# Expert-gather dots moved behind the list decode, and 80 of 128 expert blocks with a spilled first product

## The chip, the cores and the metric

The kernel runs on one core of one Trainium2 chip. The metric is the device time of one execution in microseconds, as the median of several runs. The profile shows one execution, with TensorE as PE (matmuls) and PEld (weight loads), VectorE as DVE, ScalarE as ACT, GpSimd as POOL and SyncE as SP. SP issues all plain DMAs, POOL the indirect ones.

## The reference, cut to what matters

The program is one step of a two-layer streaming encoder on 512 + 32 = 544 tokens of width 1024. Each layer has a mixer (attention, a state-space model, pooling) and then the channel mixer that this case is about, which picks 16 of 16384 experts for each of 8 heads:

```python
def one(xb):
    q = (xb @ w_q).reshape(blk, PEER_HEADS, 2, D_HALF)
    s = jnp.einsum('nhpd,hpkd->nhpk', q, sub_keys, preferred_element_type=jnp.float32)
    sv, si = lax.top_k(s, PEER_TOPK)
    ...
    cv, ci = lax.top_k(cand, PEER_TOPK)
    eid = i1 * N_KEYS + i2
    g = jax.nn.softmax(cv, axis=-1)
    act = jax.nn.gelu(jnp.einsum('nd,nhkd->nhk', xb, u_tab[eid], preferred_element_type=jnp.float32),
                      approximate=False)
    return jnp.einsum('nhk,nhkd->nd', (g * act).astype(xb.dtype), v_tab[eid])
```

So a token takes 128 experts: for each the dot of its row of `u_tab` with the token, a gelu, a gate, and the sum of rows of `v_tab` with these weights.

## The kernel before, in words

Both layers run the same code (`peer`, line 149). After the mixer and `topk` (the choice of experts, most of it on VectorE), the 544 tokens are split.

**The first 128 tokens are gathered.** For each of their 128 experts, one indirect DMA (`gather`, line 267, on POOL) brings 128 rows of 2048 floats, the u row and the v row of one expert per token, into one of three `uv` buffers. VectorE takes the dot of the u half with the tokens (`junk`, line 269), ScalarE the gelu, VectorE multiplies by the gate (line 273) and adds the weighted v half to `accg` (line 275), after which the buffer is free for the next gather.

**The other 416 tokens go through all 16384 experts densely,** in 128 blocks of 128 experts. First the gates are scattered into a dense table G: `gbuild` (the list decode, lines 404 to 421) compares the lists with an iota on VectorE (lines 406 to 411, 52 rounds of four operations of 128x1024), multiplies the one-hot matrices on TensorE (lines 417 and 418, 832 matmuls a layer), and writes G to DRAM in 13 pieces. Then for each block the first product (`upass`, line 146) multiplies the block's u rows with the tokens, in 24 matmuls of 416 columns since both sides are split in a high and a low part (`uh` by ScalarE on line 133, `ul` by VectorE on line 134); the result gets a gelu (lines 175 or 194). The second product (line 217) multiplies the gated activations with the block's v rows, again in 24 matmuls of 416 columns per block.

**Spilled blocks.** The second product needs G, the first does not. So the first `NSPILL` = 56 blocks have their first product computed ahead, while VectorE still chooses and decodes; line 176 writes the activations to the DRAM tensor `AC`. The rest, 72 blocks, are computed in the main loop (lines 184 to 234), which goes over groups of `GB` = 4 blocks, with the 14 spilled groups spread evenly between the 18 others (`order`, line 183). In a group, line 187 loads the gates, line 191 the spilled activations (or `upass` computes them), line 196 applies the gates, lines 198 and 200 split the product in `wh` and `wl`, and the loop over `d` runs the second product in eight pieces of 128 output columns. The sums of four of the eight stay in PSUM to the end; the other four are added to `acc` on VectorE (line 224), four additions a group.

**What sets the order.** A scheduler that runs when the program is built fixes the order of the instructions on each engine; the engines then work in that order. `gstep` (line 254) says how many gathers the program text issues at each place: weight `WSP` per spilled block, `WD1` per spilled group, `WD2` per other group, scaled by `GEARLY` so that the last comes a little before the end. The scheduler may draw a gather's VectorE work ahead of that. At the end `tail_load` (line 244) loads the residual rows into the three `uv` buffers and adds `accg` (line 251), and lines 230 to 234 transpose and add the dense sums.

Of the kernel before, what the change touches and what calls it, by code (L numbers as in the profile page):

```python
# [12 lines left out]
ALU = mybir.AluOpType  # L13
# [7 lines left out]
GB = 4  # L21
# [5 lines left out]
VB, WB = 4, 6  # L27
ACB = 6
UF = 1
GEARLY = 1.08  # L30
NSPILL = 56
WSP = 0.1
WD1 = 1.3
WD2 = 5
GSC = 32768.0
STARTS = [0, 16, 24, 29, 33, 36, 38, 40, 42, 43, 44, 45, 46, 47, 48, 49]
# [6 lines left out]
class Ker:  # L43
# [105 lines left out]
    def peer(s, layer):  # L149
        nc, tc, I = s.nc, s.tc, s.I  # L150
        G = s.dram.tile([ND // 32, 128, 128, 32], F32, name='G')
        AC = s.dram.tile([NSPILL, 128, ND], F32, name='AC')
        with ExitStack() as sc:
# [15 lines left out]
            with ExitStack() as gs:  # L169
                s.gbuild(gs, I1T, I2T, GhT, GlT, G)  # L170
            for b in range(NSPILL):
                ps, = s.upass(I['peer_uT'][layer, b])
                s.gstep(WSP)
                a_ = s.ac.tile([128, ND], F32, name='act')
                nc.scalar.activation(a_, ps[:, :ND], AF.Gelu)
                nc.sync.dma_start(AC[b], a_)
# [3 lines left out]
            hold = [s.psC(), s.psB(), s.psC(), s.psB()]  # L180
            un = list(range(NSPILL, 128, GB))
            sp = list(range(0, NSPILL, GB))
            order = sorted([((i - UF * (i < 2)) / len(un), g) for i, g in enumerate(un)] + [((i + 0.5) / len(sp), g) for i, g in enumerate(sp)])
            for gi, (_, g0) in enumerate(order):
# [3 lines left out]
                for b in range(g0, g0 + GB):  # L188
                    a_ = s.ac.tile([128, ND], F32, name='act')
                    if b < NSPILL:  # L190
                        nc.sync.dma_start(a_, AC[b])
                    else:
                        ps, = s.upass(I['peer_uT'][layer, b])
                        nc.scalar.activation(a_, ps[:, :ND], AF.Gelu)
                    av = a_.rearrange('p (g n) -> p g n', n=32)
                    nc.vector.tensor_mul(av, av, gt[:, :, b - g0, :])  # L196
                    wh = wp.tile([128, ND], F32R, name='wh')
                    nc.scalar.activation(wh, a_, AF.Copy)  # L198
                    wl = wp.tile([128, ND], F32R, name='wl')
                    nc.vector.tensor_sub(wl, a_, wh)  # L200
                    grp.append((wh, wl))
                for d in range(8):
                    s.gstep((WD1 if g0 < NSPILL else WD2) / 8)
                    if d % 4 == 0:
# [20 lines left out]
                    if gi == len(order) - 1:  # L225
# [5 lines left out]
                        for t, m, n in ((1, 2, 128), (3, 1, 128), (4, 1, 32)):  # L231
                            o = xs[(t - 1) // 2].rearrange('p (a b) -> p a b', a=2)[:n, (t + 1) % 2:(t + 1) % 2 + m, d * 128:(d + 1) * 128]
                            i = ps.rearrange('p (a b) -> p a b', b=128)[:n, t - 1:t - 1 + m]
# [18 lines left out]
        return xs  # L252

    def gstep(s, w):
        total = NSPILL * WSP + NSPILL // GB * WD1 + (128 - NSPILL) // GB * WD2
        s.gtot = min(NG, s.gtot + w * GEARLY * NG / total)
        while s.gdone + KP <= s.gtot:
            s.gather(s.layer, s.gdone)
            s.gdone += KP

    def gather(s, layer, s0):
        nc = s.nc
        act = s.small.tile([128, KP], F32, name='gact')
        rows = []
        for i in range(KP):
            uv = s.gp.tile([128, 2048], F32, name='uv')
            nc.gpsimd.indirect_dma_start(out=uv, out_offset=None, in_=s.I['peer_uv'].rearrange('l e d -> (l e) d'), in_offset=bass.IndirectOffsetOnAxis(ap=s.eid[:, s0 + i:s0 + i + 1], axis=0))  # L267
            junk = s.gp.tile([128, 1024], F16, name='junk', bufs=1)
            nc.vector.scalar_tensor_tensor(junk, uv[:, 0:1024], 1.0, s.xg, op0=ALU.mult, op1=ALU.mult, accum_out=act[:, i:i + 1])  # L269
            rows.append(uv)  # L270
        w = s.small.tile([128, KP], F32, name='gw')
        nc.scalar.activation(w, act, AF.Gelu)  # L272
        nc.vector.tensor_mul(w, w, s.gsl[:, s0:s0 + KP])
        for i in range(KP):
            nc.vector.scalar_tensor_tensor(s.accg, rows[i][:, 1024:2048], w[:, i:i + 1], s.accg, op0=ALU.mult, op1=ALU.add)  # L275
# [1211 lines left out]
```

## Time and profile before

| What | Value |
|---|---|
| time, median of 3 runs | 3504.01 us (3503.53 to 3505.63) |
| the profiled execution's own time | 3495.36 us |
| its span, first to last instruction | 3493.3 us |
| PE busy | 3156.7 us (90%) |
| PEld busy | 2987.6 us (86%) |
| DVE busy | 2674.9 us (77%) |
| ACT busy | 1240.8 us (36%) |
| POOL busy | 688.5 us (20%) |
| DMA | 761.07 MB, 218 GB/s over the span |
| mean granted TensorE clock | 0.946 |

The two layers follow each other; the profile's stages of the first layer are the choice of experts (about 350 to 604 us), the decode (604 to 848 us) and the main loop (871 to 1774 us), and the second layer has the same three some 1700 us later. Busy shares over the whole span mix these stages, so the tables by stretch are the ones to read. In the rows, a matmul's duration is longer than the distance to the next, since matmuls are pipelined; the distance is a stretch divided by the number of matmuls in it.

### The profile page before, as it was taken

Reading aid. Unit: us, or ns where it says so; the run is one execution under the profiler, and the core shown is the slowest. Engines: PE = TensorE matmul, PEld = TensorE weight load, DVE = VectorE, ACT = ScalarE, POOL = GpSimd, SP = SyncE. Lnnn points to the kernel's source line nnn. Section 1 sums busy time; section 2 is a strip of 40 time slices with the busy share of each in tenths; the row PEclk is TensorE's granted clock in tenths of the full one; section 3 lists DMA queues with packets and bytes.
Section 4 is the critical chain, followed back from the end, with each engine's and each line's share of the span. In section 5 each row is a group of like instructions: output and inputs, shape, how many; then the busy total and the mean of one; then the engine's idle time right before and its main releaser. Section 6 shows DMA issues by size and latency. Waiting matters only on the chain.

```text
span 3493.3 us, 48079 instructions
## 1 busy us (share of the span) xinstructions
PE 3156.7 (90%) x17932; PEld 2987.6 (86%) x17932; DVE 2674.9 (77%) x5685; ACT 1240.8 (36%) x2213; POOL 688.5 (20%) x436
## 2 busy tenths in 40 slices
PE   6779969993999999999999997799669999999998
PEld 5667868993999999999988786799569999999998
DVE  7975699998888899544455539999988988884544
ACT  3233323443333333333344422344423333333332
POOL 4432012232222222000000400133222222210000
PEclk9889989995999999999999998899779999999999
DMA  3112224998999999645432222379899999984542
GB/s 114 50 44 105 89 86 140 347 344 334 344 329 328 335 348 338 225 159 158 146 101 67 83 87 83 111 266 348 320 335 334 337 336 339 346 287 155 178 144 94
DMA packets 314437, 761.07 MB, mean 218 GB/s; under 512 B 22782, under 2 KB 164318, under 8 KB 277852
## 3 DMA queue, kind: packets, MB, share of 16 engines
q1 hardware_dynamic: 277340, 489.56, 41.3%
q0 software_dynamic: 36864, 268.45, 20.3%
q8 instruction: 140, 2.29, 0.3%
q14 instruction: 93, 0.76, 0.1%
HBM read 667.42 MB, written 90.51 MB: 217 GB/s over the span
## 4 chain that ended last, share of the span: by engine, by line
PE 51%; DVE 21%; issue 12%; DMA 10%; POOL 3%; ACT 2%; SPq 0%; POOLq 0%; ACTq 0%; DVEq 0%
PE psa L146 18%; PE psb L217 11%; PE psc L217 6%; PE psa L217 5%; DMA uv<-in_peer_uv,eid 5%; DMA raw<-in_peer_uv 4%; POOL uv L267 3%; DVE ul L134 3%; PE psa L1013 2%; DVE wl L134 1%; DVE trep L282 1%; DVE accg L275 1%; DVE X L281 1%; DVE X L284 1%; PE psa L1205 1%
## 5 line engine op out<-in xcount | busy, mean ns | idle before, releaser
L146 PE MATMUL psa<-hh,ul 128*128 128x416 f32 (+1 forms) x2304 | 805.8, 354 | 91.7 <-DVE ul L134 91.7
L146 PE MATMUL psa<-hh,uh 128*128 128x416 f32 (+1 forms) x2304 | 807.2, 354 | 10.3 <-ACT uh L133 9.6
L146 PE MATMUL psa<-hl,uh 128*128 128x416 f32 (+1 forms) x2304 | 796.8, 349 | 0.0
L267 POOL DMA_INDIRECT uv<-in_peer_uv,eid x256 | 420.4, 1642 | 1161.4 <-DVE accg L275 1010.0
L134 DVE TENSOR_TENSOR wl<-raw,wh 128x1024 fp32r<-128x1024 f32 (+1 forms) x281 | 343.6, 1224 | 270.7 <-ACT wh L133 270.1
L146 PEld LDWEIGHTS psa<-hh,ul 128*128 128x128 f32 x2304 | 439.5, 192 | 110.1 <-DVE ul L134 104.8
L133 ACT ACTIVATE uh<-raw 128x1024 fp32r<-128x1024 f32 x272 | 287.0, 1057 | 594.6 <-PE psa L146 365.3
L133 ACT ACTIVATE wh<-raw 128x1024 fp32r<-128x1024 f32 (+1 forms) x303 | 316.1, 1049 | 439.6 <-DMA raw<-in_peer_uv 357.5
L146 PEld LDWEIGHTS psa<-hh,uh 128*128 128x128 f32 x2304 | 440.4, 193 | 22.8 <-ACT uh L133 16.2
L146 PEld LDWEIGHTS psa<-hl,uh 128*128 128x128 f32 x2304 | 440.2, 192 | 5.5
L134 DVE TENSOR_TENSOR ul<-raw,uh 128x1024 fp32r<-128x1024 f32 x268 | 339.5, 1269 | 95.5 <-ACT uh L133 95.5
L217 PE MATMUL psb<-wh 128*128 128x416 f32 x1024 | 358.6, 353 | 45.8 <-ACT wh L198 45.8
L217 PE MATMUL psb<-wh,wl 128*128 128x416 f32 x1024 | 358.5, 351 | 0.0
L269 DVE SCALAR_TENSOR_TENSOR junk<-uv,xg 128x1024 f16<-128x1024 f32 x256 | 312.2, 1219 | 59.1 <-DMA uv<-in_peer_uv,eid 58.7
L217 PE MATMUL psb<-wl,wh 128*128 128x416 f32 x1024 | 357.2, 350 | 0.2 <-DVE wl L200 0.2
L275 DVE SCALAR_TENSOR_TENSOR accg<-uv,gw,accg 128x1024 f32<-128x1024 f32 x256 | 327.8, 1281 | 3.0
L217 PEld LDWEIGHTS psb<-wh 128*128 128x128 f32 x1024 | 192.9, 188 | 48.0 <-ACT wh L198 46.4
L198 ACT ACTIVATE wh<-act 128x416 fp32r<-128x416 f32 x256 | 139.0, 548 | 195.1 <-DVE act L196 131.4
L95 POOL TENSOR_TENSOR rs<-ms,nhalf 128x1 f32<-128x1 f32 (+1 forms) x35 | 19.2, 551 | 891.5 <-DVE ms L93 886.6
L217 PEld LDWEIGHTS psb<-wl,wh 128*128 128x128 f32 x1024 | 192.3, 188 | 2.6 <-DVE wl L200 0.4
L217 PEld LDWEIGHTS psb<-wh,wl 128*128 128x128 f32 x1024 | 192.1, 188 | 1.9
L272 ACT ACTIVATE gw<-gact 128x1 f32<-128x1 f32 x256 | 51.4, 201 | 373.0 <-DVE junk L269 372.3
(548 smaller groups left out, 5963.0 us busy)
## 6 DMA issues: line engine op xcount, KB each, us to landing
raw<-in_peer_uT SPq DMA_DIRECT2D x256, 512.0 KB
raw<-in_peer_uv SPq DMA_DIRECT2D x256, 512.0 KB
G<-st SPq DMA_DIRECT2D x26, 2048.0 KB
gt<-G SPq DMA_DIRECT2D x64, 832.0 KB
AC<-act SPq DMA_DIRECT2D x112, 208.0 KB
act<-AC SPq DMA_DIRECT2D x112, 208.0 KB
raw<-in_w_out SPq DMA_DIRECT2D x16, 512.0 KB
raw<-in_peer_wq SPq DMA_DIRECT2D x16, 512.0 KB
```

What stands on the lines that cost most here:

```text
L133: nc.scalar.activation(hi, raw, AF.Copy)
L134: (eng or nc.vector).tensor_sub(lo, raw, hi)
L146: nc.tensor.matmul(pss[i][:, :c - a], w[:, k, :], x[:, k, a:c], start=(k == 0 and j == 0), stop=(k == 7 and j == 2))
L198: nc.scalar.activation(wh, a_, AF.Copy)
L217: nc.tensor.matmul(ps[:, :ND], w[:, d % 4 * 128:(d % 4 + 1) * 128], x, start=(first and q == 0 and j == 0), stop=(last and q == GB - 1 and ...
L267: nc.gpsimd.indirect_dma_start(out=uv, out_offset=None, in_=s.I['peer_uv'].rearrange('l e d -> (l e) d'), in_offset=bass.IndirectOffsetOnA ...
L269: nc.vector.scalar_tensor_tensor(junk, uv[:, 0:1024], 1.0, s.xg, op0=ALU.mult, op1=ALU.mult, accum_out=act[:, i:i + 1])
L272: nc.scalar.activation(w, act, AF.Gelu)
L275: nc.vector.scalar_tensor_tensor(s.accg, rows[i][:, 1024:2048], w[:, i:i + 1], s.accg, op0=ALU.mult, op1=ALU.add)
L281: nc.vector.max_index(idx[:, 0:8], val[:, 0:8], src)
L282: nc.vector.match_replace(out=w[:n], in_to_replace=val[:, 0:8], in_values=src, imm_value=-3e38)
L1013: nc.tensor.matmul(ps[:n, :], l, ww, start=(k == 0 and i == 0), stop=(k == 7 and i == 2))
```

## The change

Three things change. The gathers' dot is put behind the most recent `wl` of the second product in VectorE's program order (`issue_after` adds an order between two instructions of one engine; no wait comes with it), where `s.gate` is set by each block of the main loop: a gather whose call stands in a group's loop has its dot behind that group's last `wl`. No gather is called in the spill loop any more, so `WSP` is gone. And 80 blocks instead of 56 are spilled, so that the main loop has 20 spilled groups and 12 others; the weights `WD1` and `GEARLY` change with it: 128 x 1.05 / 92 = 1.46 gathers per unit of weight, 2.3 per spilled group and 7.3 per other group, against 1.21, 1.6 and 6.1 before.

```diff
-GEARLY = 1.08
-NSPILL = 56
-WSP = 0.1
-WD1 = 1.3
+GEARLY = 1.05
+NSPILL = 80
+WD1 = 1.6
 WD2 = 5
...
             for b in range(NSPILL):
                 ps, = s.upass(I['peer_uT'][layer, b])
-                s.gstep(WSP)
                 a_ = s.ac.tile([128, ND], F32, name='act')
...
                     wl = wp.tile([128, ND], F32R, name='wl')
-                    nc.vector.tensor_sub(wl, a_, wh)
+                    s.gate = nc.vector.tensor_sub(wl, a_, wh).ins
                     grp.append((wh, wl))
...
     def gstep(s, w):
-        total = NSPILL * WSP + NSPILL // GB * WD1 + (128 - NSPILL) // GB * WD2
+        total = NSPILL // GB * WD1 + (128 - NSPILL) // GB * WD2
...
             junk = s.gp.tile([128, 1024], F16, name='junk', bufs=1)
-            nc.vector.scalar_tensor_tensor(junk, uv[:, 0:1024], 1.0, s.xg, op0=ALU.mult, op1=ALU.mult, accum_out=act[:, i:i + 1])
+            with s.tc.issue_after(s.gate):
+                nc.vector.scalar_tensor_tensor(junk, uv[:, 0:1024], 1.0, s.xg, op0=ALU.mult, op1=ALU.mult, accum_out=act[:, i:i + 1])
```

The changed kernel's own line numbers are one or two lower than those before. Three places show how the instructions move.

VectorE in the list decode of the first layer, before. The lines 406 to 411 are the decode, `ul` the low part of a block's u rows, `junk`, `gw` and `accg` a gather's dot, gate and sum:

```order
L406 TENSOR_TENSOR A<-iota_83,i1t 128x1024
L408 TENSOR_TENSOR B<-iota_83,i2t 128x1024
L410 TENSOR_TENSOR Ah<-A,ght 128x1024
L134 TENSOR_TENSOR ul<-raw,uh 128x1024
L269 SCALAR_TENSOR_TENSOR junk,gact<-uv,xg 128x1024
L275 SCALAR_TENSOR_TENSOR accg<-uv,gw,accg 128x1024
L410 TENSOR_TENSOR Ah<-A,ght 128x1024
L411 TENSOR_TENSOR A<-A,glt 128x1024
L406 TENSOR_TENSOR A<-iota_83,i1t 128x1024
L408 TENSOR_TENSOR B<-iota_83,i2t 128x1024
L134 TENSOR_TENSOR ul<-raw,uh 128x1024
```

The same stage in the changed kernel:

```order
L405 TENSOR_TENSOR A<-iota_83,i1t 128x1024
L407 TENSOR_TENSOR B<-iota_83,i2t 128x1024
L133 TENSOR_TENSOR ul<-raw,uh 128x1024
L410 TENSOR_TENSOR A<-A,glt 128x1024
L409 TENSOR_TENSOR Ah<-A,ght 128x1024
L405 TENSOR_TENSOR A<-iota_83,i1t 128x1024
L407 TENSOR_TENSOR B<-iota_83,i2t 128x1024
L405 TENSOR_TENSOR A<-iota_83,i1t 128x1024
L407 TENSOR_TENSOR B<-iota_83,i2t 128x1024
L410 TENSOR_TENSOR A<-A,glt 128x1024
L409 TENSOR_TENSOR Ah<-A,ght 128x1024 x2
```

Between the first and the last of the 208 decode operations there stood 31 `ul`, 29 dots and 28 sums; now there are 25 `ul` and no gather work. In both kernels 31 `ul` of dense blocks stand ahead of the decode.

VectorE from the end of the decode to the first gathers of the main loop, before (the last rows of a run of gathers, then the first group's gates, line 196, and low parts, line 200):

```order
L269 SCALAR_TENSOR_TENSOR junk,gact<-uv,xg 128x1024
L273 TENSOR_TENSOR gw<-gw,gsl 128x1
L275 SCALAR_TENSOR_TENSOR accg<-uv,gw,accg 128x1024
L196 TENSOR_TENSOR act<-act,gt 128x416 x4
L200 TENSOR_TENSOR wl<-act,wh 128x416 x4
L269 SCALAR_TENSOR_TENSOR junk,gact<-uv,xg 128x1024
L273 TENSOR_TENSOR gw<-gw,gsl 128x1
L275 SCALAR_TENSOR_TENSOR accg<-uv,gw,accg 128x1024
```

And in the changed kernel, where 27 first products follow the last decode operation:

```order
L410 TENSOR_TENSOR A<-A,glt 128x1024
L133 TENSOR_TENSOR ul<-raw,uh 128x1024 x27
L194 TENSOR_TENSOR act<-act,gt 128x416
L133 TENSOR_TENSOR wl<-raw,wh 128x1024
L198 TENSOR_TENSOR wl<-act,wh 128x416
...
L133 TENSOR_TENSOR ul<-raw,uh 128x1024 x2
L194 TENSOR_TENSOR act<-act,gt 128x416
L198 TENSOR_TENSOR wl<-act,wh 128x416
L268 SCALAR_TENSOR_TENSOR junk,gact<-uv,xg 128x1024 x2
```

All 128 gathers of a layer now have their dot in the main loop; before, 34 of them stood ahead of the first gate.

SP's queue where `tail_load` reads the residual rows into the `uv` buffers, in the first layer. Before, five such loads (line 250) stood among loads of u and v rows for groups that were still to come:

```order
L132 DMA raw<-in_peer_uv 128x2x512
L250 DMA uv<-XR 128x1024
L132 DMA raw<-in_peer_uT 128x1024
L250 DMA uv<-XR 128x1024 x2
L132 DMA raw<-in_peer_uT 128x1024
L250 DMA uv<-XR 128x1024
L250 DMA uv<-XR 32x1024
```

Now they stand at the very end, the first of them ahead of the last v load of the layer (`w_ckv` is a weight of the next layer):

```order
L131 DMA raw<-in_peer_uv 128x2x512 x4
L248 DMA uv<-XR 128x1024
L131 DMA raw<-in_peer_uv 128x2x512
L131 DMA raw<-in_w_ckv 128x576
L248 DMA uv<-XR 128x1024 x2
L131 DMA raw<-in_w_ckv 128x576 x2
L248 DMA uv<-XR 128x1024
L248 DMA uv<-XR 32x1024
```

## Rows read from the trace of the kernel before

**Rows 1.** The page: the granted TensorE clock in 40 slices of the span.

```profile
PEclk9889989995999999999999998899779999999999
```

**Rows 2.** By stretch: busy PE, PEld, DVE, ACT, POOL (instructions), clock, DMA share, GB/s.

```profile
640.00:680.00 40.00, 39.81 (x294) 36.30 (x293) 39.53 (x62) 18.66 (x35) 10.42 (x4) 1.00 0.96 363
790.00:830.00 40.00, 17.62 (x152) 14.43 (x149) 38.91 (x62) 15.91 (x30) 8.08 (x5) 0.57 0.89 349
830.00:870.00 40.00, 8.52 (x78) 7.47 (x78) 31.05 (x49) 7.26 (x18) 10.52 (x9) 0.57 0.89 327
```

**Rows 3.** Who waited for whom, 790 to 870 us: total, times, longest.

```profile
PE psb L418 <- DVE A L411: 12.7, 6, 3.9
```

**Rows 4.** VectorE's groups, 604 to 870 us: count, busy us, mean ns, idle before.

```profile
L275 DVE SCALAR_TENSOR_TENSOR accg<-uv,gw,accg 128x1024 f32<-128x1024 f32 x34 | 43.5, 1279 | 0.2
L269 DVE SCALAR_TENSOR_TENSOR junk<-uv,xg 128x1024 f16<-128x1024 f32 x34 | 41.5, 1220 | 12.9 <-DMA uv<-in_peer_uv,eid 12.9
L134 DVE TENSOR_TENSOR ul<-raw,uh 128x1024 fp32r<-128x1024 f32 x32 | 38.9, 1218 | 1.5 <-ACT uh L133 1.5
L406 DVE TENSOR_TENSOR A<-iota,i1t 128x1024 f16<-128x1024 f16 x52 | 35.6, 685 | 0.4 <-PE psc L381 0.4
```

**Rows 5.** POOL's gathers, 604 to 870 us.

```profile
L267 POOL DMA_INDIRECT uv<-in_peer_uv,eid x37 | 77.5, 2096 | 186.8 <-DVE accg L275 139.8 <-DVE gw L273 46.2 <-issue 0.8
```

**Rows 6.** First products: PE's groups, 340 to 604 us; spill gelus, first and last start.

```profile
L146 PE MATMUL psa<-hh,ul 128*128 128x416 f32 x234 | 88.8, 382 | 42.7 <-DVE ul L134 42.7
...
L175 ACT ACTIVATE act<-psa x56: 493/500/539, 411.6 to 764.9; 128x416 f32<-128x416 f32 x56
```

**Rows 7.** PE's groups, 604 to 790 us.

```profile
L146 PE MATMUL psa<-hh,ul 128*128 128x416 f32 x247 | 89.9, 365 | 1.9 <-DVE ul L134 1.9
...
L417 PE MATMUL psb<-Ah,B 128*128 128x128 f16 x183 | 28.3, 220 | 0.0
...
L417 PE MATMUL psc<-Ah,B 128*128 128x128 f16 x121 | 19.6, 220 | 0.0
```

**Rows 8.** The main loop by stretch, columns as in rows 2.

```profile
1500.00:1600.00 100.00, 100.00 (x531) 98.99 (x531) 48.30 (x65) 31.40 (x42) 0.00 (x0) 1.00 0.52 164
950.00:1400.00 450.00, 446.88 (x2355) 441.12 (x2355) 400.30 (x598) 158.31 (x274) 111.51 (x78) 1.00 0.93 336
1000.00:1100.00 100.00, 98.23 (x510) 96.38 (x510) 86.11 (x130) 35.48 (x61) 25.67 (x17) 0.98 0.93 330
```

**Rows 9.** First and last start of PE's instructions of lines 146 and 217, first layer.

```profile
L146 PE MATMUL psa<-hh,ul x544: 344/352/552, 874.2 to 1734.1; 128*128 128x416 f32 x182
L217 PE MATMUL psb<-wh x512: 344/352/716, 870.9 to 1767.5; 128*128 128x416 f32 x171
L217 PE MATMUL psa<-wh,wl x256: 344/353/356, 882.0 to 1773.5; 128*128 128x416 f32 x128
```

**Rows 10.** Groups of POOL and VectorE, 950 to 1400 us.

```profile
L267 POOL DMA_INDIRECT uv<-in_peer_uv,eid x78 | 112.3, 1440 | 338.6 <-DVE accg L275 317.7 <-DMA uv<-in_peer_uv,eid 7.9 <-DVE gw L273 7.3
...
L269 DVE SCALAR_TENSOR_TENSOR junk<-uv,xg 128x1024 f16<-128x1024 f32 x78 | 95.1, 1219 | 9.8 <-DMA uv<-in_peer_uv,eid 9.8
...
L134 DVE TENSOR_TENSOR wl<-raw,wh 128x1024 fp32r<-128x1024 f32 x63 | 76.8, 1220 | 13.5 <-ACT wh L133 13.3
...
L196 DVE TENSOR_TENSOR act<-act,gt 128x416 f32<-128x416 f32 x64 | 36.8, 586 | 2.7 <-ACT act L194 1.5 <-DMA act<-AC 1.1
```

**Rows 11.** DMA queues and issues: count and KB each.

```profile
q0 software_dynamic: 36864, 268.45, 20.3%
...
raw<-in_peer_uv SPq DMA_DIRECT2D x256, 512.0 KB
...
gt<-G SPq DMA_DIRECT2D x64, 832.0 KB
...
act<-AC SPq DMA_DIRECT2D x112, 208.0 KB
```

**Rows 12.** The residual loads of the first layer's end: first and last start.

```profile
L250 SPq DMA_DIRECT2D uv<-XR x5: 320/339/428, 1405.7 to 1415.6; - x5
```

## The prediction

> **What bounds the kernel now.** I read the page first, for the stages: the clock row has low places in the mixers and where experts are chosen, and its lowest once per layer behind that, slice 10 and again slices 29 and 30 [rows 1]. The table by stretch shows what happens in that later place. At 640 to 680 us TensorE and VectorE are both full (39.81 and 39.53 of 40 us). From 790 on VectorE stays at 38.91 of 40 us while TensorE falls to 17.62, then 8.52, at a granted clock of 0.57, so between its levels of 1.2 and 2.4 GHz and nearer the lower one [rows 2]. TensorE has run out of first products: the last spill gelu starts at 764.9 us [rows 6]. It waits for the decode's operands from VectorE [rows 3], and the main loop can't begin before G is written; its first second product is at 870.9 us [rows 9]. What holds the decode up is seen in VectorE's groups: beside 208 decode operations (four lines of 52 at 0.685 us, 142 us) and 32 `ul` it does 34 dots of 1.220 us and 34 sums of 1.279 us, 85 us of gather work [rows 4].
>
> In the main loop TensorE is the bound: 531 matmuls in 100 us, or 0.188 us each and 4.52 us per block and product, with weight loads at 98.99% [rows 8]. There the gathers cost nothing: at 950 to 1400 us, with 78 of them, TensorE is busy 446.88 of 450 us [rows 8, 10]. After some 1410 us they are used up (the residual loads that take over their buffers start at 1405.7 us [rows 12]), VectorE falls to half busy and the DMA from 336 to 164 GB/s [rows 8]. So the gathers run too early: they slow the stage that starves TensorE and are missing where they would be free.
>
> **The change, part by part,** for the first layer; the second has the same stages.
>
> *Decode.* It begins at 604 us, unchanged: 31 `ul` stand ahead of it in both orders. By then 3 x 234 matmuls are done, 29.25 blocks [rows 6]. VectorE now has 142 us of decode and 25 `ul` at 1.218, 30 us: 173 us if nothing overlaps [rows 4]. TensorE has 25 blocks at 4.52, 113 us, and 832 decode matmuls. From 604 to 790 us it did about 3 x 247 large ones, 139 us, and 2 x (183 + 121) = 608 small ones (line 418 has as many as line 417) in the remaining 47 us, so at most 0.078 us each and 65 us for 832: 178 us [rows 7]. I take 175 us, an end at 779 instead of 848. Bounds: 161 us, as VectorE's durations overlapped by some 7% in the full stretch before, and 190 us, if the two engines wait for each other.
>
> The Trainium skill, page "Perfetto Trace Analysis", section "Identifying the Most-Contended Engine", holds matmul busy time to be a poor measure of TensorE's headroom and goes by the weight loads' share. The stretch at 640 to 680 us shows 39.81 us busy but 36.30 of weight loads, 91% [rows 2]. By that rule TensorE has slack in the decode, VectorE's 161 us alone would hold, and the total would be some 28 us lower than by my 175.
>
> *First products behind it.* G is written while TensorE goes on with spilled blocks. Ahead of the first gate stand 83 `ul`; with 84 blocks done (80 and the first group) TensorE has 84 - 29.25 - 25 = 29.75 blocks left, 134 us: the main loop begins at 913 us, 42 later than now, but with 24 blocks less in it. 30 us of this cover G's last writes and the first loads, which today lie open.
>
> *Main loop.* Before, 196 block products (3 x 544 matmuls are 68 blocks, and 128 second products) took from 870.9 to the last start at 1773.5 us, 902.6 us or 4.605 each, all its small stalls included [rows 9]. Now 44 + 128 = 172 are left: 792 us, to 1705 us. This holds if VectorE and the DMA keep up.
> VectorE: per second product a `wl` of the weights, a gate, a low part and an addition, 1.220 + 3 x 0.586 = 2.98 us; 128 x 2.98 + 44 x 1.22 + 128 gathers x (1.22 + 1.28 + 0.16 for gate and read-out) = 381 + 54 + 340 = 775 us, 98% of 792. At 950 to 1400 us the same sum is 63 x 2.98 + 36 `ul` x 1.22 + 78 x 2.66 = 439 of 450, also 98%, with TensorE full [rows 8, 10].
> DMA: 48 u loads and 128 v loads of 0.524 MB, 32 gate loads of 0.852, 80 spilled activations of 0.213, 128 gathers of 268.45/256 = 1.049 MB: 271 MB in 792 us, 342 GB/s against 336 [rows 8, 11].
> Gather ring: three buffers turned over one gather in 450/78 = 5.77 us [rows 10]; needed are 792/128 = 6.19.
> So the loop now runs all along at the load of its present busiest part. Bounds: 172 x 4.52 = 778 us, or 271 MB at the 330 GB/s of the slowest of its stretches, 821 us [rows 8].
>
> *Spill traffic and gate.* 24 more writes and reads of 0.213 MB are 10 MB a layer; the writes lie beside first products alone, where little else moves, the reads are in the sum above. The gate is an order within VectorE's own queue and costs nothing by itself. Behind a dot that waits for its rows stand gates and low parts that TensorE needs: that is the second rival. POOL's queue keeps its order; the first three gathers land before the loop and then wait.
>
> *End of a layer.* The residual loads now need buffers that the last gathers free, on SP ahead of the last v load, and line 251 stands ahead of the final additions. Before they had 350 us of room [rows 12]. No row prices this; it lies between 0 and one turn of the ring, 3 x 5.77 = 17 us. I take 8, nearer the middle, since the loop ends with half a group of products already loaded.
>
> **Sum.** Per layer: 604 + 175 + 134 + 792 + 8 = 1713 against 1773 us (the last start of before), 60 us less, 120 for both. The profiled execution took 3495.4 us, 8.6 under the median; 3375 on its scale is **3384 us** as a median. A measurement of this kernel can tell about 0.2%, 7 us, from no change.
>
> **The rivals.** *The transfers become the bound.* For it: the main loop asks for 342 GB/s from end to end, in its first 95% (`GEARLY` 1.05) about 350, and the DMA share is already 0.93 [rows 8]; loads of v and gates come twice as often among spilled groups. Against it: the decode stretch moved 363 GB/s [rows 2]. At 821 us per loop each layer gains 31 us: 3442 us; with a late decode (190 us) and a full turn of the ring at the end 7 us: 3490. The Trainium skill, page "DMA: Bandwidth & Descriptors", section "Specifications", gives about 358 GB/s of HBM per core; 350 would just fit under it, and the 363 here is above it.
>
> *The ring becomes the bound, and the kernel slower.* Gathers now have only the main loop, and VectorE stops at each dot whose rows are late, with the gates of the next group behind it; TensorE then idles and loses its clock as at 790 us. Price: beside the decode a gather took 266/37 = 7.2 us [rows 5]; 128 of them are 920 us, 128 over 792, so a layer is 68 us slower and the time 3640 us. It decides from (1773 - 8 - 913)/128 = 6.66 us per gather. Against it: at the loop's own mix it was 5.77, with 9.8 us of waits for rows in 450 us [rows 10].
>
> *The decode doesn't get shorter,* because TensorE or ScalarE's evictions set its 244 us and the gathers only filled gaps: then 848 + 134 + 792 + 8 = 1782, 9 us slower per layer, 3522 us. For it: TensorE reads as full at 640 us. Against it: after 790 us TensorE is idle and VectorE still full, and the decode goes no faster [rows 2, 3].
>
> **How the numbers follow.** Forecast 65%, transfers 20%, ring 4%, no shorter decode 4%, and 7% for the forecast's lower bounds together (161, 778 and 0 us: 36 us per layer more, 3312 us). The first two and the last are faster by more than 0.2%, less 2% for a long decode and slow transfers that add up to nothing: faster 0.90, same 0.02, slower 0.08. The range leaves out half of the transfers' upper part, the two slow rivals and the extreme low end: **3322 to 3450 us**.
>
> **What would show it.** The decode's last operation near 780 us, with no dot before it; TensorE full from 604 us on at a granted clock of 1; the first second product near 913 us; about 17 gathers in each 100 us up to the end of the loop, near 1705 us; DMA near 342 GB/s there. Wrong would be: TensorE idle in the main loop behind dots that wait for rows, or behind loads of v rows; a main loop over 850 us; a decode that still ends near 848 us.

## The result, and the profile after

The changed kernel takes 3351.93 us (median; 3346.45 to 3355.85), the kernel before 3504.82 us beside it (3503.53 to 3507.74): the ratio is 0.9566, with a 95% interval of 0.955 to 0.9582. That is 153 us less. The forecast was 3384 us in a range of 3322 to 3450, so 120 us less. The execution that was profiled took 3355.85 us, 139.5 us less than the profiled execution of before.

All lines after the change stand one or two lower than before: the dot is line 268, the gather 265, the sum 274, the decode's four VectorE operations are 405 to 410, the first product is 145, the second 215, the splits 132 and 133. First the page: the slices of the granted clock.

```profile
PEclk8889988999999999999999999899999999999999
```

Slices 10, 29 and 30, at 5, 7 and 7 tenths before [rows 1], are now at 9. What stands there now, by stretch of the first layer (columns as in rows 2): the decode, the first products behind it, the main loop; below them the main loop's 450 us that rows 8 show for before.

```profile
608.00:772.00 164.00, 163.63 (x1393) 150.31 (x1392) 155.83 (x237) 88.48 (x160) 7.80 (x4) 1.00 0.77 283
780.00:904.00 124.00, 124.00 (x658) 122.87 (x658) 36.97 (x32) 42.60 (x58) 0.00 (x0) 1.00 0.56 189
904.00:1709.00 805.00, 791.98 (x4175) 778.19 (x4174) 714.29 (x1084) 283.93 (x480) 179.85 (x126) 1.00 0.93 331
950.00:1400.00 450.00, 442.26 (x2330) 434.65 (x2329) 400.85 (x605) 158.00 (x268) 101.47 (x73) 1.00 0.96 340
```

TensorE, at 8.52 of 40 us and a granted clock of 0.57 behind the old decode [rows 2], stands still for 0.4 us in all from 608 to 904 us, at 1.00. VectorE's groups from 608 to 772 us hold the decode and 25 `ul`, and no dot or sum (columns as in rows 4):

```profile
L405 DVE TENSOR_TENSOR A<-iota,i1t 128x1024 f16<-128x1024 f16 x52 | 35.7, 686 | 3.9 <-PE psb L417 2.0 <-PE psc L417 1.5 <-PE psc L380 0.4
...
L133 DVE TENSOR_TENSOR ul<-raw,uh 128x1024 fp32r<-128x1024 f32 x25 | 30.5, 1220 | 4.4 <-ACT uh L132 4.4
```

Next, the lines that answer to rows 9: first and last start of the second product, in the first layer (two rows) and in the second (two rows), and then, each from its own line's answer, the first and last decode operations, dots and residual loads.

```profile
L215 PE MATMUL psb<-wh x512: 344/352/458, 903.7 to 1704.0; 128*128 128x416 f32 x171
L215 PE MATMUL psa<-wh,wl x256: 344/352/356, 912.0 to 1709.0; 128*128 128x416 f32 x128
L215 PE MATMUL psb<-wh x512: 344/352/552, 2535.3 to 3333.5; 128*128 128x416 f32 x171
L215 PE MATMUL psa<-wh,wl x256: 344/352/356, 2543.7 to 3338.6; 128*128 128x416 f32 x128
...
L405 DVE TENSOR_TENSOR A<-iota,i1t x104: 670/685/696, 607.9 to 2398.2; 128x1024 f16<-128x1024 f16 x104
L410 DVE TENSOR_TENSOR A<-A,glt x52: 681/684/693, 616.6 to 771.5; 128x1024 f16<-128x1024 f16 x52
L268 DVE SCALAR_TENSOR_TENSOR junk<-uv,xg x128: 1211/1218/1227, 914.4 to 1691.4; 128x1024 f16<-128x1024 f32 x128
L248 SPq DMA_DIRECT2D uv<-XR x5: 327/339/425, 1687.0 to 1697.2; - x5
```

So the decode runs from 607.9 to 772.2 us, 164.3. The first second product comes at 903.7, 33 us later than before; the last starts at 1709.0, 64.5 us earlier. The main loop went from 902.6 to 805.3 us. In the second layer, rows of before for the same line give 2571.9 and 3477.9: there the loop went from 906.0 to 803.3 us. From the last start in layer one to the last in layer two it was 1704.4 us and is 1629.6, 74.8 us less. 64.5 + 74.8 = 139.3 us, which is the whole gain of the profiled executions.

The row of the dots among VectorE's waits in the main loop, 904 to 1709 us (total, times, longest), shows that the dots, though they all run there now, hardly wait for rows:

```profile
DVE junk L268 <- DMA uv<-in_peer_uv,eid: 9.3, 6, 2.6
```

### The profile page after: what moved, and what is told of

It reads as the page before. It is cut to its first block, busy times and chain, and to the rows that moved or that the text cites. A ratio compares the mean times of both kernels' runs of the same rounds, so it can differ in the third digit from the quotient of the medians.

```text
span 3354.1 us, 48383 instructions
## 1 busy us (share of the span) xinstructions
PE 3123.9 (93%) x17932; PEld 2960.0 (88%) x17932; DVE 2665.7 (79%) x5685; ACT 1245.7 (37%) x2215; POOL 644.0 (19%) x436
## 4 chain that ended last, share of the span: by engine, by line
PE 48%; issue 22%; DVE 20%; DMA 7%; ACT 2%; POOL 1%; SPq 0%; POOLq 0%; ACTq 0%; DVEq 0%
PE psa L145 12%; PE psb L215 12%; PE psc L215 6%; PE psa L215 6%; DMA raw<-in_peer_uv 4%; PE psa L1012 3%; DVE ul L133 2%; DVE wl L133 1%; DMA uv<-in_peer_uv,eid 1%; DMA act<-AC 1%; DVE trep L281 1%; DVE accg L274 1%; DVE junk L268 1%; DVE X L280 1%; DVE X L283 1%
## 5 line engine op out<-in xcount | busy, mean ns | idle before, releaser
L145 PE MATMUL psa<-hh,uh 128*128 128x416 f32 (+1 forms) x2304 | 805.3, 353 | 8.5 <-ACT uh L132 8.4
L265 POOL DMA_INDIRECT uv<-in_peer_uv,eid x256 | 376.5, 1471 | 1770.5 <-DVE accg L274 1673.5
L215 PE MATMUL psc<-wh 128*128 128x416 f32 x512 | 180.1, 352 | 4.9 <-ACT wh L132 4.9
```

The costliest lines, as they stand in the source:

```text
L145: nc.tensor.matmul(pss[i][:, :c - a], w[:, k, :], x[:, k, a:c], start=(k == 0 and j == 0), stop=(k == 7 and j == 2))
L215: nc.tensor.matmul(ps[:, :ND], w[:, d % 4 * 128:(d % 4 + 1) * 128], x, start=(first and q == 0 and j == 0), stop=(last and q == GB - 1 and ...
```

## The experiments

One measure serves them all. A block product is 24 matmuls, and the fully busy stretch of before [rows 8] gives 4.52 us for it. The loop's *loss* is its time less 4.52 us for each block product in it: TensorE's idle time, slower matmuls behind a stop, and the 24 to 32 other matmuls that fall into the loop. All stages are those of the first layer, from the first second product to the last. The kernel before took 3505.0 us beside e1 to e4, 3508.6 beside e5 to e8 and 3510.3 beside e9 to e12, and the ratios are to these.

| kernel | first 2nd product at | loop | block products | loss | time | ratio (95%) |
|---|---|---|---|---|---|---|
| before | 870.9 | 903 | 196 | 17 | 3504.82 | 1 |
| changed | 903.7 | 805 | 173 | 23 | 3351.93 | 0.9566 (0.955 to 0.9582) |
| e1 gate, 56 | 798.0 | 933 | 196 | 47 | 3395.40 | 0.9674 (0.9646 to 0.9701) |
| e2 no gate, 80 | 927.5 | 816 | 172 | 38 | 3404.37 | 0.9701 (0.9675 to 0.9728) |
| e3 changed, no gathers | 904.9 | 805 | 173 | 23 | 3349.93 | 0.9549 (0.9512 to 0.9585) |
| e4 half rows | 900.0 | 837 | 173 | 55 | 3413.50 | 0.973 (0.9694 to 0.9766) |
| e5 gate, 72 | 864.0 | 832 | 181 | 14 | 3347.49 | 0.9544 (0.9518 to 0.9569) |
| e6 gate, 64 | 832.6 | 894 | 189 | 39 | 3384.77 | 0.9637 (0.9607 to 0.9666) |
| e7 earlier gate | 923.2 | 814 | 172 | 36 | 3409.75 | 0.9722 (0.9695 to 0.9749) |
| e8 e1, no gathers | 795.7 | 915 | 196 | 29 | 3367.12 | 0.9596 (0.9562 to 0.9629) |
| e9 gate, 72 again | 866.1 | 836 | 181 | 18 | 3347.79 | 0.954 (0.952 to 0.9559) |
| e10 changed again | 901.8 | 803 | 173 | 21 | 3352.46 | 0.955 (0.9536 to 0.9564) |
| e11 gate, 76 | 883.9 | 817 | 177 | 17 | 3343.88 | 0.9524 (0.9507 to 0.954) |
| e12 gate, 96 | 972.8 | 778 | 157 | 69 | 3457.55 | 0.9858 (0.984 to 0.9876) |

In the second layer the same measure gives 21 us for the changed kernel, 20.5 for e5 and 25 for e2, so a few us between two rows of the table decide nothing.

### One half of the change at a time (e1, e2)

**e1** keeps the gate and goes back to 56 spilled blocks, with the gathers' spread for 56:

```
-GEARLY = 1.05
-NSPILL = 80
-WD1 = 1.6
+GEARLY = 1.08
+NSPILL = 56
+WD1 = 1.3
```

> The gate alone: 56 spilled blocks and the weights of before, dots behind the low parts, no gathers in the spill loop. Its order has 25 first products in the decode and 4 behind it ahead of the first gate, and no gather before the main loop. My theory (the time goes wherever TensorE runs out of work, and a decode without gathers is short enough that 60 blocks nearly cover it): decode over near 772 us, TensorE through with its 60 blocks near 798 us, first second product near 800 us, main loop 196 block products at 4.6 us, end near 1702 us, so about 3340 us (3320 to 3365). Rival 1, the decode's length decides and the spill count is only filler: also 3340 to 3360. Rival 2, the spill count is what fills TensorE's gap and the gathers beside the decode were harmless: no gain, 3490 to 3510 us.

**e2** keeps 80 blocks and takes the gate away; gathers are again issued beside the spilled blocks:

```
+WSP = 0.1
...
+                s.gstep(WSP)
...
-                    s.gate = nc.vector.tensor_sub(wl, a_, wh).ins
+                    nc.vector.tensor_sub(wl, a_, wh)
...
-        total = NSPILL // GB * WD1 + (128 - NSPILL) // GB * WD2
+        total = NSPILL * WSP + NSPILL // GB * WD1 + (128 - NSPILL) // GB * WD2
...
-            with s.tc.issue_after(s.gate):
-                nc.vector.scalar_tensor_tensor(junk, ...)
+            nc.vector.scalar_tensor_tensor(junk, ...)
```

> 80 spilled blocks alone: no gate, gathers called in the spill loop as before. Its order has 40 first products, 28 dots and 27 sums inside the decode, 12 first products and 10 dots behind it. My theory: the decode stays long (about 250 us, end near 850 us), but TensorE has 40 blocks and the decode's matmuls in it, 246 us, so it is never out of work; first second product near 917 us, main loop 172 block products at 4.55 us with 90 gathers, end near 1700 us: about 3335 us (3320 to 3365). Rival 1 (the decode's length decides): 76 us later per layer than the change, 3490 to 3510 us. Rival 2 (the spill count): 3340 to 3360.

Each half alone gives some two thirds of the whole: 110 us and 100 us, against 153 together. They remove the same idle time in two ways. In e1 the decode takes 164.3 us as in the changed kernel, and the second products begin 27 us behind it. In e2 the decode is as long as before, but TensorE has enough first products to fill it. e2 by stretch (columns as in rows 2): decode, first products.

```profile
605.00:853.00 248.00, 240.75 (x1787) 223.66 (x1785) 238.32 (x363) 114.26 (x222) 78.94 (x31) 0.99 0.91 344
853.00:927.00 74.00, 67.47 (x356) 65.07 (x355) 51.55 (x70) 24.82 (x46) 19.43 (x14) 0.95 0.99 371
```

TensorE is busy 240.75 of 248 us, where before it stood at 17.62 and 8.52 of 40 at the end of the same decode [rows 2]. The 7 us it stands there, and the 7 of the next 74, are e2's own; the changed kernel has none of them. Both expectations were too low, since both kernels also lose more in the main loop: 47 and 38 us against 23. The rivals that saw no gain (3490 to 3510 us) are out for both. The gathers' weights `GEARLY` and `WD1` change along with the number of blocks and weren't tried by themselves. e1's loop, first by stretch, then the dots' waits on VectorE and the waits for `ul` on TensorE (all 798 or 800 to about 1731 us):

```profile
798.00:1731.00 933.00, 907.39 (x4735) 885.84 (x4735) 744.15 (x1108) 317.04 (x527) 165.03 (x126) 0.99 0.85 294
```

```profile
DVE junk L268 <- DMA uv<-in_peer_uv,eid: 47.4, 37, 3.4
...
PE psa L145 <- DVE ul L133: 10.2, 9, 2.1
```

The dots wait 47.4 us for rows (9.3 in the changed kernel), and TensorE waits 9 times for a `ul`, 10.2 us in all. One such place in e1's timeline, VectorE, then TensorE (start, duration; in brackets the idle time before it and what ended it):

```profile
1371.86 1.23 DVE L268 SCALAR_TENSOR_TENSOR junk<-uv,xg 128x1024 f16<-128x1024 f32 x1 [2.22 <-DMA uv<-in_peer_uv,eid]
...
1373.55 1.28 DVE L274 SCALAR_TENSOR_TENSOR accg<-uv,gw,accg 128x1024 f32<-128x1024 f32 x1
1374.76 1.22 DVE L133 TENSOR_TENSOR wl<-raw,wh 128x1024 fp32r<-128x1024 f32 x1
1375.89 1.22 DVE L268 SCALAR_TENSOR_TENSOR junk<-uv,xg 128x1024 f16<-128x1024 f32 x1
...
1377.04 1.22 DVE L133 TENSOR_TENSOR ul<-raw,uh 128x1024 fp32r<-128x1024 f32 x1
```

```profile
1378.31 0.46 PE L145 MATMUL psa<-hh,ul 128*128 128x416 f32 x1 [2.14 <-DVE ul L133]
...
1379.33 0.55 PE L145 MATMUL psa<-hh,uh 128*128 128x416 f32 x1
1379.68 0.55 PE L145 MATMUL psa<-hl,uh 128*128 128x416 f32 x1
```

A dot waits 2.22 us for its rows; behind it stand a sum, a `wl`, a second dot, and only then the `ul` that TensorE needs. TensorE stands 2.14 us.

### Do the gathers cause the loop's loss? (e3, e8, e4)

**e3** is the changed kernel without gathers, dots and sums; **e8** is e1 without them:

```
-        while s.gdone + KP <= s.gtot:
+        while False and s.gdone + KP <= s.gtot:
```

> The changed kernel without any gather: the experts of the first 128 tokens are left out. Prices what the gathers still cost in the main loop, where a block product took 805/172.7 us, 4.66, against 4.52 in a stretch without gathers. My theory: main loop about 781 us instead of 805, nothing else moves, 3304 us (3295 to 3315). Rival, the main loop's loss has nothing to do with gathers (loads of v rows, gates, spilled activations): 3340 to 3355 us.

> The gate-alone kernel (56 blocks) without any gather (the experts of the first 128 tokens are left out). Its main loop took 933 us, 48 more than 196 block products at 4.52 us, with VectorE standing 47 us at dots for rows. Theory A: without dots the loss falls to what the 80-block kernel without gathers had, 17 to 25 us, so 3345 us (3330 to 3355). Rival C (the 56-block order loses time for other reasons, loads of u and v rows that come late): stays at 3380 to 3395 us.

e3's loop by stretch:

```profile
905.00:1709.00 804.00, 795.86 (x4182) 779.11 (x4181) 412.83 (x573) 262.59 (x354) 0.55 (x1) 1.00 0.54 165
```

In e3 VectorE's work falls from 714 to 413 us and the transfers from 331 to 165 GB/s, and the loop takes the same 805 us. So in the changed kernel 128 gathers of 1.049 MB with their dots and sums cost no time that shows: 3349.93 against 3351.93 us, with intervals that overlap. That is the rival's range (3340 to 3355 us); the forecast of 3304 missed.

The two losses of 23 us are of equal size but not the same loss. Without gathers the scheduler lays VectorE's other instructions in another order as well, and TensorE stops at other places. In the changed kernel 9 of its 13 us of idle time are waits for parts of a second product's weights, `wh` and `wl`; in e3 none is. Its stops are at `uh`, the high part of the u rows for a first product. First TensorE's waits in e3, 905 to 1709 us, then ScalarE before one of them:

```profile
PE psa L145 <- ACT uh L132: 6.4, 9, 3.2
```

```profile
1184.89 1.06 ACT L132 ACTIVATE wh<-raw 128x1024 fp32r<-128x1024 f32 x1 [4.33 <-DMA raw<-in_peer_uv]
...
1186.30 1.04 ACT L132 ACTIVATE uh<-raw 128x1024 fp32r<-128x1024 f32 x1
```

The `uh` stands in ScalarE's queue behind the high part of a v row that ScalarE awaited for 4.33 us, and likewise, with 4 to 5 us, at all nine stops. So e3 shows what the gathers cost on balance; it doesn't show that VectorE's load and the transfers have no part in the changed kernel's 23 us.

With 56 blocks the gathers do cost something: e1 without them loses 29 in place of 47 us, and at 3367.12 us e8 lies between its two expectations. TensorE's stops there are of the kind of e3's, 9.7 us at `uh` and 4.0 at `ul`; the rest of the 29 is not traced.

**e4** gathers half a row, from a table of `u` rows alone:

```
-            nc.gpsimd.indirect_dma_start(out=uv, ..., in_=s.I['peer_uv'].rearrange(...), ...)
+            nc.gpsimd.indirect_dma_start(out=uv[:, 0:1024], ..., in_=s.I['peer_ug'], ...)
...
-            nc.vector.scalar_tensor_tensor(s.accg, rows[i][:, 1024:2048], ...)
+            nc.vector.scalar_tensor_tensor(s.accg, rows[i][:, 0:1024], ...)
```

> The changed kernel with gathers of the u half alone (4 KB instead of 8 KB per row, from a table of u rows; the sum takes the u half, so the v half is left out): every instruction stays, the gathers' bytes are halved, 67 MB less per layer. If the main loop's loss against 4.52 us per block product comes from the transfers: main loop about 785 us, 3312 us (3300 to 3325). If it comes from VectorE's or the ring's order: 3340 to 3355 us.

It was to be faster or the same, and it was slower by 62 us than the changed kernel. e4's loop by stretch, then the waits of VectorE and TensorE, 904 to 1737 us:

```profile
900.00:1737.00 837.00, 806.11 (x4177) 786.57 (x4175) 709.58 (x1085) 281.64 (x480) 174.64 (x126) 0.98 0.75 240
```

```profile
DVE junk L268 <- DMA uv<-in_peer_ug,eid: 51.5, 32, 4.1
...
PE psa L145 <- DVE ul L133: 19.9, 10, 3.9
```

With half the bytes (240 GB/s) the dots wait longer for their rows, 51.5 us against 9.3. The edit changed the order in which the scheduler lays VectorE's queue as well as the bytes, so it doesn't price the bytes. The gathers landed sooner (5.7 us in the median, 8.4 in the changed kernel) at three quarters of the transfer load, so the 32 us more a layer most likely come from the order; no run changed the order alone.

### How many blocks (e5, e6, e9 to e12)

The changed kernel with `NSPILL` at 72, 64, 76 and 96 in place of 80; nothing else differs.

> The changed kernel with 72 spilled blocks instead of 80: 19 first products behind the decode instead of 27, still none of the gathers there. Theory A (what is left is the main loop's loss against 4.52 us per block product, and it depends on how the fixed order of VectorE fits, with dots that stand before their rows are in: 24 us a layer with 80 blocks, 48 with 56): between the two, 3355 to 3370 us. Rival B (the loss comes from the load of the main loop, which has 128 gathers in 805 us with 80 blocks and 841 us with 72): less loss, 3335 to 3345 us.

> The changed kernel with 64 spilled blocks: 11 first products behind the decode; the main loop may begin near 835 us. Theory A: nearer to the run with 56 blocks and the gate, 3370 to 3395 us. Rival B (load of the main loop): 3325 to 3340 us.

> The changed kernel with 72 spilled blocks instead of 80, as in e5, in more rounds and beside the changed kernel itself on the same chip. In e5 it read 3347.5 (ratio 0.9544), the changed kernel 3351.9 (0.9566), with intervals that overlap. Theory A (the first second product starts 36 us earlier, the main loop has eight more block products: both amount to the same work on TensorE, and what differs is only how many dots stand ahead of their rows): within 0.3% of the changed kernel, 3340 to 3355. Theory B (fewer blocks behind the decode leave less to do at its edge, so 72 is really better): below 3342 and below e10 by more than 0.2%.

> The changed kernel as it is, again, on the same chip as e9, e11 and e12: 3346 to 3356, ratio 0.955 to 0.958. It is the measure for the three others.

> The changed kernel with 76 spilled blocks. Theory A (the loss of the main loop is smooth in the number of blocks; 64 lost 40 to 47 us of it, 72 lost 14 to 21, 80 lost 22 to 24): between 72 and 80, 3340 to 3360. Theory B (the loss is set by how the order of VectorE and of the issues happens to fall, as the misses of e1, e4, e6 and e7 suggest): it may lie anywhere between 3335 and 3390, with no smooth path through 72, 76, 80.

> The changed kernel with 96 spilled blocks: 43 first products behind the decode in place of 28, so the first second product at about 775 + 43 x 4.6 = 973 us of the span, and 157 block products in the main loop. Theory A (TensorE stays the bound): 157 x 4.65 = 730 us, the layer ends at 1703 as with 80, 3345 to 3360. Theory B (the 128 dots and gathers of the layer crowd into a loop that is 75 us shorter: VectorE has 128 x 1.22 + the rest = some 700 us of work there, and the same gathers and the 16 more blocks read back ask over 345 GB/s): the main loop takes 770 to 790 us, the layer ends at 1745 to 1765, 3420 to 3470.

e10 read as expected; e6, e9 and e11 came as their theory A had it (e11 also within theory B), e12 as its theory B; e5 fell between its two. From 72 to 80 the time is flat within 0.3%. On one chip, five runs each, 76 read 3336.65 to 3346.99 us and the changed kernel 3348.06 to 3353.72: 76 is the fastest kernel tried, by 8.6 us in the medians, and no run of one lies among those of the other. With 72 the runs overlap with both. At 64 and 56 the loop's loss is 39 and 47 us instead of 14 to 23. At 96 it is 69 us. e12's loop by stretch, then who waited for whom on TensorE (973 to 1752 us) and ScalarE (976 to 1690 us), and the same of ScalarE in the changed kernel:

```profile
1000.00:1700.00 700.00, 666.08 (x3475) 649.38 (x3474) 632.75 (x965) 239.68 (x409) 186.82 (x115) 1.00 0.96 344
```

```profile
PE psb L215 <- ACT wh L132: 22.5, 12, 2.8
PE psa L228 <- DVE uv L232: 17.0, 1, 17.0
...
ACT wh L132 <- DMA raw<-in_peer_uv: 40.1, 26, 5.2
...
ACT wh L132 <- DMA raw<-in_peer_uv: 66.2, 34, 4.7
```

Here the loop is short for what has to come through in it: 344 GB/s at a share of 0.96 of the DMA engines. Its loss stands in two places. At the end of the layer TensorE waits once for 17.0 us. It needs a buffer that a final addition (line 232) has to read first, this addition needs the residual rows, and their loads start only at 1734.3 us, since the last gathers (last dot at 1737.1) still hold the `uv` buffers. A gather takes 5.9 us from dot to dot there, about what the ring of three buffers took before (5.77). That points to the ring, the prediction's second rival, and it is the prediction's term for the end of a layer at its upper bound.

In the loop TensorE waits 22.5 us for the high part of weights (3.9 in the changed kernel). The transfers as the bound, the first rival, aren't shown by that. ScalarE waits for rows of `v` longer in the changed kernel, which loses a third as much, and of the 12 late `wh` only one was split from a row that had just come in. The others follow, on ScalarE, an instruction that waited for a second product, a gate or a dot, as here (TensorE goes on at 1225.0 us, after 2.50 us of idle time):

```profile
1221.95 0.55 ACT L196 ACTIVATE wh<-act 128x416 fp32r<-128x416 f32 x1 [5.97 <-PE psb L215]
...
1223.88 1.04 ACT L132 ACTIVATE wh<-raw 128x1024 fp32r<-128x1024 f32 x1
```

Order and load may both have a share in it; the two weren't separated.

### The gate one step earlier (e7)

The gate is the last decode operation instead of a low part, so that the dots may run beside the 28 first products that follow the decode:

```
-                    s.gate = nc.vector.tensor_sub(wl, a_, wh).ins
+                    nc.vector.tensor_sub(wl, a_, wh)
...
-                nc.vector.tensor_tensor(A, A, bc(GlT), op=ALU.mult)
+                s.gate = nc.vector.tensor_tensor(A, A, bc(GlT), op=ALU.mult).ins
```

> The changed kernel with the gate set by the decode's last operation of each round instead of by the main loop's low parts: dots still come behind the decode, but 26 of them may now stand among the first products behind it, where VectorE was busy 41 of 130 us. First second product still near 904 us. Theory A: the main loop's loss isn't set by how many gathers it holds (without any gather it was the same 805 us), so 3340 to 3360 us, with dots that wait for rows deciding within that. Rival B: 102 gathers instead of 128 in the loop, loss nearly gone, 3315 to 3335 us.

Both expectations missed: 3409.75 us, 58 slower than the changed kernel. e7's first products by stretch:

```profile
770.00:923.00 153.00, 140.79 (x751) 136.34 (x749) 110.69 (x152) 51.43 (x96) 45.45 (x28) 0.97 0.94 351
```

In the changed kernel VectorE and the DMA had room behind the decode (36.97 of 124 us; a share of 0.56, 189 GB/s). Gathers put there raise the DMA to 0.94 and 351 GB/s, and TensorE, full there before, falls to 140.79 of 153 us. Most of that is one stop, for a `uh` whose u row ScalarE awaited for 11.21 us (ScalarE, then TensorE):

```profile
810.50 1.06 ACT L132 ACTIVATE uh<-raw 128x1024 fp32r<-128x1024 f32 x1 [11.21 <-DMA raw<-in_peer_uT]
...
811.61 0.72 PE L145 MATMUL psa<-hh,uh 128*128 128x416 f32 x1 [7.83 <-ACT uh L132]
```

What these gathers bring is not got back: the loop has fewer of them and still loses 36 us. They don't come more thinly, though: 99 dots from 924.5 to 1513.8 us are one in 6.0 us, against 6.1 in the changed kernel. So e7 didn't try a loop with a lighter load of gathers.

## Why the prediction held, and where its terms were off

**What bounds the kernel** held. TensorE ran out of first products before the decode was done, and the main loop had room for the gathers. e1 and e2 each fill that hole in one way, and each brings two thirds of the gain. e3 shows the second half: without the gathers, which are spread over the whole loop, the time is 2 us less, and that is within the noise.

**Decode**, 175 forecast, 164.3 measured. The term that was mis-sized is the price of the small decode matmuls, "at most 0.078 us each", taken at its upper end. It was what the large ones left of 186 us, 3.8 us of idle time included, shared out over the small ones. The timeline of the changed kernel inside the decode, TensorE and VectorE, shows the starts:

```profile
660.34 0.22 PE L417 MATMUL psb<-A,B 128*128 128x128 f16 x1
660.40 0.22 PE L416 MATMUL psb<-Ah,B 128*128 128x128 f16 x1
...
661.15 0.22 PE L416 MATMUL psc<-Ah,B 128*128 128x128 f16 x1
...
661.44 0.35 PE L145 MATMUL psa<-hh,ul 128*128 128x416 f32 x1
661.63 0.35 PE L145 MATMUL psa<-hh,uh 128*128 128x416 f32 x1
```

```profile
660.31 0.68 DVE L405 TENSOR_TENSOR A<-iota,i1t 128x1024 f16<-128x1024 f16 x1
660.91 0.68 DVE L407 TENSOR_TENSOR B<-iota,i2t 128x1024 f16<-128x1024 f16 x1
```

Small matmuls start every 0.058 us (660.34 to 661.15, 14 steps), large ones every 0.19. Per column that is the same, so 0.188 us for 416 columns [rows 8] would have given the price: 0.188 x 128/416 = 0.058. 832 x 0.058 + 600 x 0.189 = 162 us for TensorE. VectorE's operations of 0.685 us start every 0.60, so they overlap by 0.08: 208 x 0.60 + 25 x 1.14 (the `ul` at 664.52 is followed at 665.66) = 153 us, and it stands some 8 us more, about half of it until TensorE frees its operands and half until a `uh` is there. So the decode took what TensorE needed, 163.63 of 164 us, with VectorE some 5% below it. Of the two values weighed in the prediction the lower one, 161 us, was the better.

The Trainium skill's rule that gave it (page "Perfetto Trace Analysis", section "Identifying the Most-Contended Engine") reads weight loads at 150.31 of 164 us, 92%, as headroom on TensorE. The size came out as by the rule; the headroom didn't: the trace has 0.4 us of gaps between matmuls there, and TensorE's own sum is 162 us.

**First products**, 134 forecast, 131.5 measured (772.2 to 903.7): 28.5 blocks at 4.52 us, one fewer than counted, and some 2 us of decode matmuls that were still due.

**Main loop**, 792 forecast, 805.3 measured. The term that was mis-sized is the price of a block product, 4.605 us from before's whole loop; it came to 805.3 / 173 = 4.655. 8.6 us are that price, 4.6 are one block more than counted. That the new loop runs "all along at the load of its present busiest part" was right, but the load doesn't explain the price. Before's 450 us at that load went at 4.59 us per block product (2355 matmuls [rows 8]), the same 450 us of the changed kernel at 4.64 (2330), and e3, without the load, has the same loss at other stops. Most of TensorE's idle time in the loop is waits for `wh` and `wl`; what would take them away is open. The 98% reckoned for VectorE is a sum of durations that overlap: it was busy 400.30 of the 450 us [rows 8], 89%, and is now 714.29 of 805.

**End of a layer**, 8 forecast. The residual loads did move behind the last gathers, to 1687.0 to 1697.2 us, but they landed before the last second product. From its start to the last of the final additions it was 3.5 us before and is 4.6 now, so the term is about 1 here; in e12 it is 17.0.

```profile
L232 DVE TENSOR_TENSOR uv<-psa,uv x24: 269/274/425, 1698.2 to 1713.6; 128x256 f32<-128x256 f32 x8, 128x128 f32<-128x128 f32 x8, 32x128 f32<-32x128 f32 x8
```

**The sum.** In the first layer 4 us later at the start (607.9 for 604), 11 less for the decode, 2 less for the first products, 13 more in the loop and 8 less at the end: 1709 instead of 1713, 64.5 us less than before. That it comes so near is in part luck, as 21 us of terms that were too long and 17 of terms that were too short cancel. The second layer, taken as the first, gained 74.8: there before's decode and loop were 4 and 3 us longer, and the changed kernel's loop was 2 us shorter. The other 13 us between 139.5 and 153 are that before's profiled execution lay 9.5 under its median and after's 4 over its own.

**The rivals.** The transfers as the bound didn't come at 80 blocks (331 GB/s, and no time less without gathers); at 96, with 344 GB/s, they aren't shown to be it. The ring as the bound and a slower kernel: gathers took 805/128 = 6.3 us each, under the 6.66 from which it decides, and VectorE stood 9.3 us at dots. At 96 blocks the 17.0 us at the end of a layer fit it. Its mechanism, a dot that waits and keeps back the operands behind it, is what e1's timeline shows, and it goes with some of the losses: TensorE's waits for `ul` are 1.4 us in the changed kernel and 10.2, 12.5 and 19.9 in e1, e6 and e4, which lose 47, 39 and 55. It doesn't go with the others: in e2, e7 and e12 TensorE waits 0.6 to 4.2 us for `ul`, and 11.6, 11.7 and 22.5 for a `wh` from ScalarE. A decode that doesn't get shorter fell with its first row.

**What stays open.** e5, with 72 blocks, has dots that wait 42.1 us and a loop that loses 14; its waits on VectorE and TensorE, 864 to 1697 us, are:

```profile
DVE junk L268 <- DMA uv<-in_peer_uv,eid: 42.1, 32, 2.8
...
PE psa L145 <- DVE ul L133: 1.8, 2, 1.3
```

So the dots' waits as such don't set the loss. That it hangs on what stands behind them, and so on the scheduler's order, is argued from e1's timeline and not shown: no run here changed the order by itself. Nor is it traced why rows of `v` come late without gathers, at half the transfer load (e3, e8).

## What to carry to other kernels

Two edits that fill the same hole aren't worth the sum of their gains: price the idle time once, and then look for what the second edit adds elsewhere (here 43 to 52 us, much of it in the loop that follows). Before work is put on an engine that runs its queue in order, see what will stand behind it when its data are late; a free half of that engine is no proof that the work fits there, and in e7 the u rows then came late. When a count like the spilled blocks is set, try its neighbours: 72 to 80 were equal within 0.3%, 64 and 96 cost 1% and 3%.

## What the runs showed of the hardware beyond that

A short stop of TensorE can cost more than its length. In e1, soon after the 2.14 us of idle time before 1378.31 us, matmuls start 0.35 us apart instead of 0.19, and the stretch behind it reads a granted clock of 0.58, between the levels of 1.2 and 2.4 GHz and nearer the lower; the next one reads 1.00 again. e1 by stretch, then the changed kernel behind a stop of 1.81 us that ended at 1366.56:

```profile
1379.00:1383.00 4.00, 4.00 (x15) 3.88 (x14) 3.38 (x5) 2.38 (x5) 1.05 (x1) 0.58 0.98 379
1383.00:1387.00 4.00, 4.00 (x23) 3.95 (x22) 3.41 (x5) 2.72 (x4) 0.00 (x0) 1.00 1.00 396
...
1367.00:1371.00 4.00, 4.00 (x24) 3.96 (x23) 3.69 (x6) 1.71 (x3) 0.43 (x2) 1.00 0.78 280
```

The slow stretch of e1 has 15 matmuls where the one behind it has 23: eight fewer, at 0.19 us each, are 1.5 us on top of the 2.1. The idle time that a profile puts before an instruction is thus not all that such a wait costs, and busy time can't show the rest. Not every stop does this: behind that of the changed kernel the clock stays at 1.00.

The transfers also went higher than the main loop's 331 to 344 GB/s: 371 over 74 us in e2, and 396 over 4 us here. The Trainium skill, page "DMA: Bandwidth & Descriptors", section "Specifications", gives about 358 GB/s of HBM per core; e2's stretch is above it, so here that figure was no ceiling.
